# One streaming-encoder layer on one core: w_out's load and split, the sample's output tile and bank L's release are put later in the last stage

## The chip, the cores and the metric

The kernel runs on one core of a Trainium2 chip. The metric is the device time of one launch in microseconds (us), median of three runs. A profiled execution gives the rows below.

## The reference

One layer for two request groups that share weights: a prompt of 2048 frames and a sample of 8 streams with 16 new frames each (cut to what matters):

```python
hq, hf, hi, hgate, fq, fk, fv, fgate, fflog, mq, mgate = _split_in(x @ w_in)
forget = lb + (1 - lb) * sigmoid(hf)
o_hg, hg_new = _hgrn2(state, silu(hq), 1 - forget, hi, log(forget))     # gated recurrence, 4 heads of 128
o_fx = _fox(fq, fk, fv, cumsum(log_sigmoid(fflog + b)))                 # causal softmax attention with a forget bias
o_mem = _cross(mq, mem_k, mem_v)                                        # attention into 256 memory tokens
mix = concat([rmsnorm(o_hg) * silu(hgate), o_fx * silu(fgate), o_mem * silu(mgate)])
y = layernorm(DN_ALPHA * x + mix @ w_out)
```

All in float32. The kernel makes each float32 product from three products of a high and a low part (names ending in h/hi and l/lo).

## The kernel before

The first two thirds of the span project x by w_in (tiles `pj`), spill the results to DRAM (`s_q`, `s_f`, `s_kk` and so on), do the sample's attention and recurrence, and begin the prompt's attention. At about 1009 us of the span the last stage starts. It holds, for 16 tiles of 128 frames: the recurrence (`hgrn_tile`: PSUM banks `L` and `M`, work tile `hQK`, mask tile `hC`), the attention into memory (`cross`: `cqg`, `cP`), the rest of the prompt's attention (`fox`, from the sixth step of its third block of 512 frames on: keys `fk`, queries `fq`, probabilities `fP`, sums `facc`, output `pv`), and the output projection (`out_tile`: bank `o`, weights `woh`/`wol`, row tile `y`), first for the sample ("s", whose mix `ms` POOL fetches from `s_ms`), then for the 16 prompt tiles.

`drive` writes the order of TensorE's work in this stage. Each of those generators is a `Stream`; a `yield` gives the shape of its next matmuls, their planned time, a chain of things that must come first (`("D", 0.7)`: 0.7 us planned on VectorE; `("A", ..)`: ScalarE; `("M", t)`: t us of plain waiting; a third entry names a bank freed when that link ends) and the banks it takes. The plan keeps its own clock and picks a ready stream. It knows neither the DMA queues nor the split of w_out. The order on the other engines is made by the framework from the order of the code and its own planned times; each engine runs its instructions in that order and stops at the first one that has to wait. So does the SP queue with its DMA issues.

One tile of the recurrence does its masked products level by level: three groups of matmuls into `L` (slots 0 and 1 in one group of width 64, then slots 2 and 3), then into `M`. Between two levels VectorE multiplies `hQK` by the running products `P` (L713), and copies the finished slots into `hC` (`pick`, L721 and L723). The forget values `hF` have one buffer: the next tile's are asked for when this tile has used its own. A tile t of the recurrence may begin when output tile t-3 is done (`AHEAD = 3`).

w_out (8 blocks of 128 rows, 512 KB each) comes through the two buffers of `y`, the same ring that `out_tile` uses: each block is cast to `woh` on ScalarE (L1148) and the rest to `wol` on VectorE (L1149), in two halves; block k+2 is asked for when block k is split.

Of the kernel before, what the change touches and what calls it, by code (L numbers as in the profile page):

```python
# [89 lines left out]
def kernel(  # L90
# [185 lines left out]
    def finish(gen):  # L276
        for _ in gen:
            pass
# [403 lines left out]
    def hgrn_tile(t, hb, psh, psl, hstate, emit_mix, bufs, psm=None):  # L682
# [18 lines left out]
        L = psl()  # L701
# [28 lines left out]
        for slot, b in enumerate((2, 4, 8) if smp else (2, 4, 8, 16), 2):  # L730
            P = update(b // 2, P)
            side = [("D", -0.25)] * 2
            if slot == 3:
                pick(0, 1)
                side = [("D", -0.55)]
            elif slot == 4:
                pick(2)
            elif slot == 5:
                pick(3)
            if slot == 5:  # L740
                yield 32, 0.3, [("D", 0.7), ("D", -0.3), ("D", -0.2, "L")], {}
            else:
                yield 32, 0.3, [("D", 0.7), ("D", -0.3)] + side, {"M": 1} if slot == 4 else {}
            if slot == 4:
                M = (psm or psh)()
            for h in range(4):
                for i in range(4):
                    c = slice(32 * i, 32 * i + 32)
                    d = L[c, h, slot, :] if slot < 4 else M[c, h, 32 * slot - 128 : 32 * slot - 96]
                    mm(d, K[:, h, c], Q[:, h, c])  # L750

        if not smp:
            P = update(16, P)
            pick(4)
            yield 32, 0.3, [("D", 0.7), ("D", -0.45)], {}
            for h in range(4):
                for i in (0, 2):
                    c = slice(32 * i, 32 * i + 32)
                    d = slice(32 * i + 32, 32 * i + 64)
                    mm(M[64 + 16 * i : 96 + 16 * i, h, 64:96], K[:, h, c], Q[:, h, d])  # L760
            P = update(32, P)
            pick(5)
            A = diag[t % 2]
            for i in range(4):
                c = slice(32 * i, 32 * i + 32)
                ACT.copy(A[c, :, c], C[c, :, :])
            yield 64, 0.5, [("D", 0.7), ("D", -0.4), ("A", -1.0)], {}
            for h in range(4):
                mm(M[0:64, h, 64:128], K[:, h, 0:64], Q[:, h, 64:128])
            P = update(64, P)  # L770
            ACT.copy(A[0:64, :, 64:128], M[0:64, :, 64:128])
            ACT.copy(A[0:32, :, 32:64], M[64:96, :, 64:96])
            ACT.copy(A[64:96, :, 96:128], M[96:128, :, 64:96])
        else:
            P = update(8, P)
            pick(3, 4)
            A = tl([128, 4, 128], "hA", 1)
            DVE.tensor_tensor(out=A.rearrange("p h (i t) -> p h i t", t=32),
                              in0=C.unsqueeze(2).to_broadcast([128, 4, 4, 32]),
                              in1=bm3.unsqueeze(1).to_broadcast([128, 4, 4, 32]), op=ALU.mult)  # L780
# [203 lines left out]
    def fox(n):  # L984
        T0 = 512 * n
        c0 = T0 if n < 2 else T0 + 128
        for pr in range(2):
            hs = slice(2 * pr, 2 * pr + 2)
            q1 = fp.tile([68, 2, 512], F32R, name="fq1", bufs=1)
            POOL.dma_start(q1[0:64], s_qq[0:64, hs, T0 : T0 + 512])  # L990
            POOL.dma_start(q1[64:68], s_m[:, n, pr])
            q2 = fp.tile([128, 2, 512], F32R, name="fq2", bufs=1)
            POOL.dma_start(q2, s_qq[:, hs, T0 : T0 + 512])
            pv = pf.tile([128, 512], F32, name="pv")
            acc = [fp.tile([128, 512], F32, name=f"facc{hh}", bufs=1) for hh in range(2)]
            def values(V, st, t0, PT, first, last):
                for hh in range(2):
                    r = slice(64 * hh, 64 * hh + 64)
                    mm(pv[r, t0:], V[:, st, r], PT[hh][:, t0:], start=first, stop=last)
                if not first:  # L1000
                    for hh in range(2):
                        DVE.tensor_tensor(out=acc[hh][:, t0:], in0=acc[hh][:, t0:], in1=PT[hh][:, t0:], op=ALU.add)  # L1002

            for c in range(n + 1):
                V = fp.tile([128, 4, 128], F32, name="fV")
                SP.dma_start(V, s_fv[512 * c : 512 * c + 512, 128 * pr : 128 * pr + 128]
                             .rearrange("(j p) c -> p j c", p=128))
                for duo in (0, 2):
                    cs = slice(512 * c + 128 * duo, 512 * c + 128 * duo + 256)
                    k1 = fp.tile([68, 2, 256], F32R, name="fk1", bufs=2)  # L1010
                    POOL.dma_start(k1, s_kk[64:132, hs, cs])  # L1011
                    k2 = fp.tile([128, 2, 256], F32R, name="fk2", bufs=2)
                    POOL.dma_start(k2, s_kk[0:128, hs, cs])
                    PTs, us, wait = [], 0.0, []
                    for st in (duo, duo + 1):
                        t0 = 128 * st if c == n else 0
                        first = c == 0 and st == 0
                        size = (512 - t0) / 512
                        us += size
                        sl = slice(128 * (st % 2), 128 * (st % 2) + 128)  # L1020
                        yield 128, 0.95 * size + 0.1 * (c == n), wait + [("M", 3.0 if first else 0.1)], {"f": 2}
                        PT = []
                        for hh in range(2):
                            ps = ptf()
                            mm(ps[:, t0:], k1[:, hh, sl], q1[:, hh, t0:], start=True, stop=False)
                            mm(ps[:, t0:], k2[:, hh, sl], q2[:, hh, t0:], start=False, stop=(c < n))
                            if c == n:
                                mm(ps[:, t0 : t0 + 128], identb, cstb, start=False, stop=True)
                            pT = acc[hh] if first else fp.tile([128, 512], F32, name="fP", bufs=B_FP)
                            ACT.activation(pT[:, t0:], ps[:, t0:], AF.Exp)  # L1030
                            PT.append(pT)
                        PTs.append((st, t0, PT, first, c == n and st == 3))
                        wait = [("A", 0.1 + 0.5 * size, "f"), ("A", 0.1 + 0.5 * size, "f")]
                    yield 64, 0.95 * us, wait, {}
                    for args in PTs:
                        values(V, *args)
            yield 64, 1.0, [("D", 0.7)] * 3, {"f": 1}, lambda: have["O"] >= 4 * ((2 * n + pr - 3) // 2)
            lp = ptf()
            for hh in range(2):
                mm(lp[64 * hh : 64 * hh + 64, :], ones[:, 0:64], acc[hh])  # L1040
            rl = fp.tile([128, 512], F32, name="fP", bufs=B_FP)
            ACT.activation(rl, lp, AF.Ln)
            ACT.activation(rl, rl, AF.Exp, scale=-1.0)
            DVE.tensor_tensor(out=rl, in0=pv, in1=rl, op=ALU.mult)
            gt = fp.tile([128, 512], F32, name="fP", bufs=B_FP)
            SP.dma_start(gt, s_fg[pr, :, c0 : c0 + 512])
            DVE.tensor_tensor(out=gt, in0=gt, in1=rl, op=ALU.mult)
            mixF[n, pr] = tuple(fp.tile([128, 512], F32R, name=f"mixF{i}", bufs=5) for i in range(2))
            split_mix(mixF[n, pr][0], mixF[n, pr][1], gt)
            yield None, 0.0, [("A", 0.6, "f"), ("A", 0.6), ("D", 0.7), ("D", 0.7), ("A", 0.6), ("D", 0.7)], {}  # L1050
        fox_done[0] = n + 1
# [174 lines left out]
    def out_tile(t):  # L1226
# [14 lines left out]
        for half in range(2):  # L1241
            c = slice(512 * half, 512 * half + 512)
            for k in range(8):
                yield 128, 0.71, [("D", 0.7, "o"), ("D", -0.7)] if half and not k else [], {} if k else {"o": 1}
                if k == 0:
                    ps = ptile("o", B_O)
                mm(ps, lhs(0, k), woh[:, k, c], start=(k == 0), stop=False)
# [76 lines left out]
    def outs():  # L1324
        for t in ["s"] + list(range(16)):
            need["O"] = t
            yield from out_tile(t)
            have["O"] = 0 if t == "s" else t + 1
# [8 lines left out]
    def drive():  # L1337
        h = Stream(hgrn_tiles(0), lambda: busy[0] < have["O"] + AHEAD)
        g = Stream(hgrn_tiles(1), lambda: busy[1] < have["O"] + AHEAD)
        x = Stream(crosses(), lambda: have["C"] < have["O"] + AHEAD)  # L1340
        f = Stream(fox_gen)
        o = Stream(outs(), out_ready)
        shape = 128
        while any(s.live for s in (h, g, x, f, o)):
# [25 lines left out]
    for a in range(2):  # L1370
        for i in range(2):
            POOL.dma_start(ms[a][i], s_ms[i, 4 * a : 4 * a + 4].rearrange("k p t -> p k t"))
    finish(load_w_out())
    with tc.manual_schedule(engines={PE.engine}):
        drive()

# [71 lines left out]
```

## Time and profile before

| what | value |
|---|---|
| median of 3 runs | 1562.55 us (1560.22 to 1562.56) |
| profiled execution, device time | 1558.94 us |
| its span from first to last instruction | 1557.1 us |
| TensorE busy | 1440.6 us (93% of the span) |
| VectorE, ScalarE, GpSimd busy | 755.0, 506.8, 169.3 us |
| mean granted TensorE clock | 0.973 |

Busy time of TensorE is that of pipelined matmuls, so 93% is not 93% of its peak. Idle time of another engine costs nothing unless TensorE comes to wait for it.

### The profile page before, as it was taken

Reading aid. Unit: us, or ns where it says so; the run is one execution under the profiler, and the core shown is the slowest. Engines: PE = TensorE matmul, PEld = TensorE weight load, DVE = VectorE, ACT = ScalarE, POOL = GpSimd, SP = SyncE. Lnnn points to the kernel's source line nnn. Section 1 sums busy time; section 2 is a strip of 40 time slices with the busy share of each in tenths; the row PEclk is TensorE's granted clock in tenths of the full one; section 3 lists DMA queues with packets and bytes.
Section 4 is the critical chain, followed back from the end, with each engine's and each line's share of the span. In section 5 each row is a group of like instructions: output and inputs, shape, how many; then the busy total and the mean of one; then the engine's idle time right before and its main releaser. Section 6 shows DMA issues by size and latency. Waiting matters only on the chain.

```text
span 1557.1 us, 29616 instructions
## 1 busy us (share of the span) xinstructions
PE 1440.6 (93%) x12119; PEld 1170.7 (75%) x12119; DVE 755.0 (48%) x1531; ACT 506.8 (33%) x1168; POOL 169.3 (11%) x221
## 2 busy tenths in 40 slices
PE   7999999999998999889899989869998999999997
PEld 7999997996996688768787976626666766666665
DVE  4522232211333155546565323248776667777664
ACT  4323321311333221121111233346553544555441
POOL 0710000000001110000010023211111011011000
PEclk9999999999999999999999999979999999999999
DMA  7655349568668886585452375594644344444221
GB/s 247 208 146 165 132 161 302 196 202 278 213 224 256 257 251 193 159 248 176 131 144 85 128 161 117 121 242 120 163 112 120 104 108 107 134 107 112 78 76 61
DMA packets 219527, 254.71 MB, mean 164 GB/s; under 512 B 40190, under 2 KB 165310, under 8 KB 219392
## 3 DMA queue, kind: packets, MB, share of 16 engines
q1 hardware_dynamic: 165984, 217.32, 44.3%
q0 software_dynamic: 53408, 35.51, 11.0%
q8 instruction: 95, 1.56, 0.4%
q14 instruction: 40, 0.33, 0.1%
HBM read 199.55 MB, written 53.12 MB: 162 GB/s over the span
## 4 chain that ended last, share of the span: by engine, by line
PE 62%; DMA 17%; DVE 10%; issue 5%; ACT 3%; POOL 2%; SPq 1%; DVEq 0%; ACTq 0%; POOLq 0%
PE pj L122 32%; PE o L122 9%; PE f L122 4%; DMA wraw<-in_w_feat_dram 4%; PE pv L122 3%; PE h L122 3%; DMA rb<-s_r 2%; PE dv L122 2%; PE ds L122 2%; DMA fk<-s_kk 2%; PE M L122 2%; DMA hF<-s_f 2%; DMA xr<-in_x_feat_dram 1%; DVE hQK L713 1%; DMA fq1m<-s_qq 1%
## 5 line engine op out<-in xcount | busy, mean ns | idle before, releaser
L122 PE MATMUL pj<-xh,whi 128*128 128x384 f32 (+1 forms) x1056 | 362.4, 343 | 2.2 <-DVE lo L355 1.4
L122 PE MATMUL pj<-xh,wlo 128*128 128x384 f32 (+1 forms) x1056 | 350.2, 332 | 0.2 <-DVE wlo L262 0.2
L122 PE MATMUL pj<-xl,whi 128*128 128x384 f32 (+1 forms) x1056 | 349.5, 331 | 0.0
L122 PEld LDWEIGHTS pj<-xh,whi 128*128 128x128 f32 x1056 | 201.5, 191 | 27.3 <-issue 19.2
L122 PEld LDWEIGHTS pj<-xl,whi 128*128 128x128 f32 x1056 | 201.3, 191 | 4.8 <-issue 1.2
L122 PEld LDWEIGHTS pj<-xh,wlo 128*128 128x128 f32 x1056 | 200.7, 190 | 3.5 <-issue 2.9
L307 ACT ACTIVATE e<-pj 128x384 f32<-128x384 f32 (+1 forms) x96 | 45.3, 473 | 348.4 <-PE pj L122 307.0
L950 DVE TENSOR_REDUCE fmx<-pj 128x1 f32<-128x512 f32 (+3 forms) x160 | 96.3, 609 | 78.0 <-PE pj L122 77.0
L122 PE MATMUL pj<-whi,xh 128*128 128x256 f32 (+1 forms) x408 | 122.2, 300 | 12.2 <-ACT whi L261 8.6
L262 DVE TENSOR_TENSOR wlo<-wraw,whi 128x1024 fp32r<-128x1024 f32 (+1 forms) x60 | 75.3, 1255 | 117.3 <-ACT whi L261 116.9
L1002 DVE TENSOR_TENSOR facc<-facc,fP 128x512 f32<-128x512 f32 (+3 forms) x144 | 83.1, 600 | 92.1 <-ACT fP L1030 61.3
L122 PE MATMUL pj<-wlo,xh 128*128 128x256 f32 (+1 forms) x408 | 117.8, 289 | 0.2 <-DVE wlo L262 0.2
L122 PE MATMUL pj<-whi,xl 128*128 128x256 f32 (+1 forms) x408 | 117.7, 289 | 0.0
L122 PE MATMUL f<-fq,fk 68*128 68x512 f32 (+4 forms) x320 | 94.6, 408 | 22.6 <-DMA fk<-s_kk 13.6
L122 PEld LDWEIGHTS pj<-whi,xh 128*128 128x128 f32 x408 | 79.3, 195 | 28.0 <-issue 13.7
L261 ACT CAST whi<-wraw 128x1024 fp32r<-128x1024 f32 (+1 forms) x60 | 62.8, 1046 | 106.5 <-DMA wraw<-in_w_feat_dram 100.6
L1030 ACT ACTIVATE fP<-f 128x512 f32<-128x512 f32 (+3 forms) x144 | 72.1, 524 | 75.0 <-PE f L122 74.1
L122 PEld LDWEIGHTS f<-fq,fk 68*128 68x128 f32 (+1 forms) x320 | 56.8, 201 | 41.3 <-issue 13.9
L122 PE MATMUL pj<-fk1m,fq1m 66*128 66x512 f32 (+3 forms) x160 | 64.3, 404 | 19.5 <-DVE fmx L950 9.6
L1011 POOL DMA_DIRECT2D fk<-s_kk x40 | 39.9, 997 | 386.7 <-PE f L122 333.3
L122 PEld LDWEIGHTS pj<-wlo,xh 128*128 128x128 f32 x408 | 79.8, 196 | 1.9 <-issue 0.8
L122 PEld LDWEIGHTS pj<-whi,xl 128*128 128x128 f32 x408 | 79.5, 195 | 1.8 <-issue 0.8
(304 smaller groups left out, 2352.7 us busy)
## 6 DMA issues: line engine op xcount, KB each, us to landing
kv<-in_cache_fox_k_dram SPq DMA_DIRECT2D x64, 512.0 KB
kv<-in_cache_fox_v_dram SPq DMA_DIRECT2D x64, 512.0 KB
wraw<-in_w_feat_dram SPq DMA_DIRECT2D x56, 512.0 KB
fk<-s_kk POOLq DMA_DIRECT2D x40, 256.0 KB, 4.6
xr<-in_x_feat_dram SPq DMA_DIRECT2D x34, 256.0 KB
rb<-s_r SPq DMA_DIRECT2D x32, 256.0 KB
y<-in_x_prompt_dram SPq DMA_DIRECT2D x16, 512.0 KB
out_dram<-y SPq DMA_DIRECT2D x16, 512.0 KB
```

Source lines behind the costliest of these rows:

```text
L122: PE.matmul(out, lhsT=lhsT, rhs=rhs, start=start, stop=stop)
L261: pin(ACT.copy(hi[:, r, :w], raw[:, :, :w]))
L262: pin(DVE.tensor_tensor(out=lo[:, r, :w], in0=raw[:, :, :w], in1=hi[:, r, :w].bitcast(F32), op=ALU.subtract))
L307: ACT.activation(e, ps, AF.Sigmoid)
L713: DVE.tensor_tensor(out=qk, in0=qk, in1=by, op=ALU.mult)
L950: DVE.tensor_reduce(out=mx[:, hh, tt, c : c + 1], in_=ps, axis=AX.X, op=ALU.max)
L1002: DVE.tensor_tensor(out=acc[hh][:, t0:], in0=acc[hh][:, t0:], in1=PT[hh][:, t0:], op=ALU.add)
L1011: POOL.dma_start(k1, s_kk[64:132, hs, cs])
L1030: ACT.activation(pT[:, t0:], ps[:, t0:], AF.Exp)
```

## The change

```diff
             if slot == 5:
-                yield 32, 0.3, [("D", 0.7), ("D", -0.3), ("D", -0.2, "L")], {}
+                yield 32, 0.3, [("D", 0.7), ("D", -0.3), ("D", -0.3)], {}
...
             P = update(16, P)
             pick(4)
-            yield 32, 0.3, [("D", 0.7), ("D", -0.45)], {}
+            yield 32, 0.3, [("D", 0.7), ("D", -0.2, "L"), ("D", -0.3)], {}
...
-                        yield 128, 0.95 * size + 0.1 * (c == n), wait + [("M", 3.0 if first else 0.1)], {"f": 2}
+                        yield 128, 0.95 * size + 0.1 * (c == n), wait + [("M", 6.0 if first else 0.1)], {"f": 2}
...
-                yield 128, 0.71, [("D", 0.7, "o"), ("D", -0.7)] if half and not k else [], {} if k else {"o": 1}
+                yield 128, 0.71, [("D", 0.7, "o"), ("D", -0.7)] if half and not k else [("M", 20.0)] if t == "s" and not k else [],\
+                    {} if k else {"o": 1}
...
         f = Stream(fox_gen)
+        finish(load_w_out())
         o = Stream(outs(), out_ready)
...
-    finish(load_w_out())
     with tc.manual_schedule(engines={PE.engine}):
         drive()
```

Four things: the plan frees bank `L` one level later in a tile; the first step of each head pair of the prompt's attention is planned 6 us instead of 3 us after the one before; the first half of the sample's output tile is planned 20 us after its stream is made (its second half keeps the old chain); and the code that loads and splits w_out stands behind the first steps of the recurrence, cross and attention streams, which issue their first loads.

SP queue, from the last two loads ahead of the stage on (`lng`, `lnb`: the layer norm's weights; `y<-in_w_out_dram`: w_out's blocks; `hQK`, `hV`: tile 1 of the recurrence; `cqg`: tile 0 of cross):

```order
 L1130 DMA lng<-in_ln_g_dram 128x1024
 L1131 DMA lnb<-in_ln_b_dram 128x1024
+L694 DMA hQK<-s_q 128x4x128
+L696 DMA hV<-s_v 128x512
+L1183 DMA cqg<-s_mq 128x2x128
+L1184 DMA cqg<-s_mg 128x2x128
 L1140 DMA y<-in_w_out_dram 128x1024 x2
-L694 DMA hQK<-s_q 128x4x128
-L696 DMA hV<-s_v 128x512
-L1183 DMA cqg<-s_mq 128x2x128
-L1184 DMA cqg<-s_mg 128x2x128
-L850 DMA hG<-s_g 128x4x128
```

The first pair of w_out's blocks moves behind four loads; behind the pair now come `fV`, `hG` and tile 1's `hF`, and only then the second pair. On POOL the order stays: four loads of `ms`, then the `fk` loads.

TensorE at the start of the stage, before:

```order
L122 MATMUL pv<-fP,fV 64x512 x3
L122 MATMUL o<-woh,mixHh 128x512
L122 MATMUL o<-wol,mixHh 128x512
L122 MATMUL o<-woh,mixHl 128x512
L122 MATMUL f<-fq_9411,fk_9590 128x512
L122 MATMUL f<-fq_9414,fk_9592 128x512
```

and with the change:

```order
L122 MATMUL pv<-fP,fV 64x512 x3
L122 MATMUL f<-fq_9411,fk_9542 128x512
L122 MATMUL f<-fq_9414,fk_9544 128x512
...
L122 MATMUL L<-hQK 32x64 x16
L122 MATMUL f<-mkT,cqg 128x256 x4
L122 MATMUL L<-hQK 32x32 x16
L122 MATMUL pv<-fP,fV 64x512 x4
L122 MATMUL L<-hQK 32x32 x16
```

The scores of a new key tile (`fk_9590` before, `fk_9542` now, the same load; eight rows in all, before in two lots of four with `o` rows between) come straight behind `pv`; the sample's first `o` matmul stands 30 rows later than it did.

VectorE in the middle of tile 0's levels, before (`P_9674`, `P_9701`, `P_9735` are the products of its second to fourth update):

```order
L713 TENSOR_TENSOR hQK<-hQK,P_9674 128x2x64x4
L723 COPY_PREDICATED hC<-cb,L 128x128
L1149 TENSOR_TENSOR wol<-y,woh 128x512 x2
L723 COPY_PREDICATED hC<-cb,L 128x128
L1149 TENSOR_TENSOR wol<-y,woh 128x512 x2
L713 TENSOR_TENSOR hQK<-hQK,P_9701 128x2x32x8
L1002 TENSOR_TENSOR facc_9417<-facc_9417,fP 128x512
L1002 TENSOR_TENSOR facc_9418<-facc_9418,fP 128x512
L713 TENSOR_TENSOR hQK<-hQK,P_9735 128x2x16x16
L1250 SCALAR_TENSOR_TENSOR y<-y,o 128x512
```

and with the change (`P_9768` and `P_9790` are the last two updates of tile 0):

```order
L1149 TENSOR_TENSOR wol<-y,woh 128x512 x4
L723 COPY_PREDICATED hC<-cb,M 128x128
L1002 TENSOR_TENSOR facc_9417<-facc_9417,fP 128x512
L713 TENSOR_TENSOR hQK<-hQK,P_9768 128x2x8x32
L723 COPY_PREDICATED hC<-cb,M 128x128
L713 TENSOR_TENSOR hQK<-hQK,hF 128x2x256
L1002 TENSOR_TENSOR facc_9418<-facc_9418,fP 128x512
L1219 TENSOR_TENSOR cqg<-h,cqg 128x256
L1149 TENSOR_TENSOR wol<-y,woh 128x512 x2
L679 TENSOR_TENSOR mixMl<-cqg,mixMh 128x256
L1149 TENSOR_TENSOR wol<-y,woh 128x512 x2
L713 TENSOR_TENSOR hQK<-hQK,P_9790 128x2x4x64
```

Before, the last of the 16 halves of the split stood ahead of tile 0's third update; now the second pair stands ahead of its fifth and the third pair ahead of its sixth update, and the fourth pair behind that, in the levels of tile 1.

## Rows read from the trace of the kernel before

**Rows 1.** The page's slices: the TensorE clock that was granted in each of 40 equal slices of the span (38.9 us each), in tenths, and the mean busy share of the DMA engines.
```profile
PEclk9999999999999999999999999979999999999999
DMA  7655349568668886585452375594644344444221
```

**Rows 2.** Four stretches of the stage: window, its length, busy us (and instructions) of TensorE, its weight loads, VectorE, ScalarE, GpSimd; granted clock, DMA share, GB/s.
```profile
1016.00:1040.00 24.00, 13.71 (x31) 4.66 (x31) 9.65 (x20) 7.91 (x13) 6.38 (x8) 0.78 1.12 275
1040.00:1060.00 20.00, 16.90 (x237) 10.42 (x238) 17.14 (x34) 13.81 (x31) 1.71 (x2) 0.76 0.56 166
1060.00:1500.00 440.00, 412.63 (x4646) 295.93 (x4642) 310.75 (x676) 217.47 (x647) 45.00 (x55) 0.98 0.41 112
1500.00:1557.00 57.00, 45.38 (x364) 34.73 (x364) 32.42 (x56) 12.68 (x43) 0.00 (x0) 0.98 0.18 65
```

**Rows 3.** TensorE's instructions in order of time from 1025 us on: start, us, line, tile, count, and in brackets the idle time before and what ended it.
```profile
1025.25 1.93 PE L122 MATMUL pv<-fP,fV 128*64 128x512 f32 x6
1027.94 0.49 PE L122 MATMUL o<-woh,mixHh 128*128 128x512 f32 x1 [0.76 <-ACT woh L1148]
1028.67 0.49 PE L122 MATMUL o<-wol,mixHh 128*128 128x512 f32 x1 [0.23 <-DVE wol L1149]
1029.46 0.49 PE L122 MATMUL o<-woh,mixHl 128*128 128x512 f32 x1 [0.30 <-DMA mixHl<-s_ms]
1037.31 0.80 PE L122 MATMUL f<-fq,fk 68*128 68x512 f32 x1 [7.36 <-DMA fk<-s_kk]
1039.20 1.65 PE L122 MATMUL f<-fq,fk 128*128 128x512 f32 x3 [1.09 <-DMA fk<-s_kk]
...
1046.63 0.46 PE L122 MATMUL L<-hQK 128*32 128x32 f32 x32 [0.50 <-DVE hQK L713]
1047.44 0.50 PE L122 MATMUL o<-woh,mixHh 128*128 128x512 f32 x1 [0.36 <-ACT woh L1148]
1048.51 0.50 PE L122 MATMUL o<-wol,mixHh 128*128 128x512 f32 x1 [0.56 <-DVE wol L1149]
...
1050.06 0.79 PE L122 MATMUL o<-woh,mixHh 128*128 128x512 f32 x1 [0.82 <-ACT woh L1148]
...
1052.80 0.66 PE L122 MATMUL L<-hQK 128*32 128x32 f32 x32 [0.79 <-DVE hC L723]
...
1066.94 0.40 PE L122 MATMUL o<-woh,mixHh 128*128 128x512 f32 x1
1067.18 0.39 PE L122 MATMUL o<-wol,mixHh 128*128 128x512 f32 x1
```

**Rows 4.** VectorE's instructions in order of time, the same columns.
```profile
1027.92 2.50 DVE L1149 TENSOR_TENSOR wol<-y,woh 128x512 fp32r<-128x512 f32 x4 [1.24 <-DMA hQK<-s_q]
1040.66 0.69 DVE L1002 TENSOR_TENSOR facc<-facc,fP 128x512 f32<-128x512 f32 x1 [10.24 <-ACT fP L1030]
```

**Rows 5.** The issues of the `fk` loads on POOL in order of time, and what the instructions of line 1013 (the larger of the two loads of a key tile) show from issue to landing in 1015 to 1045 us.
```profile
1020.28 1.01 POOL L1011 DMA_DIRECT2D fk<-s_kk  x1
1021.28 0.73 POOL L1013 DMA_DIRECT2D fk<-s_kk  x1
DMA to landing us min/median/max: 15.9/16.9/17.9
```

**Rows 6.** SP's DMA issues in order of time.
```profile
1017.73 1.03 SPq L1140 DMA_DIRECT2D y<-in_w_out_dram  x2
...
1027.22 0.36 SPq L1006 DMA_DIRECT2D fV<-s_fv  x1
1029.24 15.73 SPq L1140 DMA_DIRECT2D y<-in_w_out_dram  x4
1046.60 0.38 SPq L695 DMA_DIRECT2D hF<-s_f  x1
```

**Rows 7.** The DMA queues in 1016 to 1040 us (q1 is SP's, q0 is POOL's): packets, MB, share of 16 engines; and the size of a w_out issue and of an `hF` issue in the list of issues.
```profile
q1 hardware_dynamic: 3513, 4.81, 73.1%
q0 software_dynamic: 3647, 1.77, 39.1%
y<-in_w_out_dram SPq DMA_DIRECT2D x8, 512.0 KB
hF<-s_f SPq DMA_DIRECT2D x17, 256.0 KB
```

**Rows 8.** A piece of the chain that ended last: start, us, what.
```profile
1044.64 4.73 DMA y<-in_w_out_dram
```

**Rows 9.** The stretches of 4 us in which the granted clock fell a second time, columns as in rows 2.
```profile
1048.00:1052.00 4.00, 2.67 (x5) 1.08 (x5) 3.02 (x7) 2.14 (x5) 0.00 (x0) 0.68 0.70 224
1052.00:1056.00 4.00, 3.21 (x39) 2.66 (x39) 3.82 (x13) 3.88 (x9) 0.66 (x1) 0.50 0.35 131
```

**Rows 10.** What TensorE waited for in 1060 to 1557 us: who, for whom, us in total, times, longest.
```profile
PE L L122 <- DVE hC L723: 26.4, 14, 4.8
PE o L122 <- DVE y L1250: 3.4, 7, 0.9
PE M L122 <- DVE hC L723: 0.9, 2, 0.5
PE h L1209 <- ACT hkT L787: 0.2, 1, 0.2
```

**Rows 11.** All engines in order of time around the longest of those waits.
```profile
1187.35 0.70 DVE L713 TENSOR_TENSOR hQK<-hQK,hF 128x512 f32<-128x512 f32 x1
...
1195.28 0.69 DVE L697 TENSOR_TENSOR hQK<-hQK,hF 128x512 f32<-128x512 f32 x1 [4.00 <-DMA hF<-s_f]
1198.08 0.66 PE L122 MATMUL L<-hQK 128*32 128x32 f32 x32 [4.82 <-DVE hC L723]
```

## The prediction

> **What bounds the kernel now.** The granted clock over the span comes first: one slice of forty is below 9 tenths, and there the DMA engines are at their busiest of the last third [rows 1]. It is the start of the last stage, the place that the change touches. Next the stage by stretches: from 1016 to 1040 us TensorE is busy 13.71 of 24 us at a clock of 0.78, from 1040 to 1060 us 16.90 of 20 at 0.76; after that it is 94% busy (412.63 of 440) at 0.98 [rows 2]. So the stage is TensorE's, with a hole of some 13 us at its start and small waits behind. TensorE's rows in order of time tell what the hole is: the last `pv` is through at 1027.2, three `o` matmuls of the sample follow with short waits on the split of w_out, and then it waits 7.36 and 1.09 us for a key tile `fk`; from 1046 to 1053 us come five more waits, three on the split (0.36, 0.56, 0.82) and two in the recurrence (0.50, 0.79) [rows 3]. The `fk` load had been issued at 1021.28 and took 15.9 to 17.9 us [rows 5], because 6.6 MB moved in those 24 us at 275 GB/s [rows 2, 7]. VectorE stood idle for 10.24 us for the same load, after it had split w_out's first pair of blocks in 2.50 us [rows 4]. Last the waits of the rest: 26.4 us in 14 waits of an `L` group on `hC`, 3.4 us on `y`, 1.1 us others [rows 10].
>
> **Bank L's release.** It moves a planned time, so only rows in TensorE's order. The 26.4 us look as if they were meant, but one wait for each of the 14 tiles left says something else: it is the third `L` group of a tile, behind its own tile's first two `pick`s, not the next tile's first group. The plan lets a tile begin when an output tile ends, so two tiles overlap in `L` only at the start of the stage. I take 0 for the 14 waits (bounds: 26.4 gained if they did follow the release, 0), since nothing ahead of the third group is edited.
>
> **The fox wait of 6.** It puts a head pair's first scores 3 us later in the plan, past other matmuls that are ready. Among the waits after 1060 us none is on a query or key load [rows 10], so there is nothing to gain; other work covers it: 0.
>
> **w_out and the sample's tile.** Seven terms, all against the profiled execution (1558.94 us, span 1557.1, 1.84 around it); the sum is a difference and is then put on the median, 1562.55, which lies 3.6 above.
>
> 1. Three waits for the split inside 1047 to 1051 us go, since no `o` stands there: 0.36 + 0.56 + 0.82 = -1.7 [rows 3]. The waits ahead of the first three `o` (0.76, 0.23, 0.30) gain nothing: TensorE then waits for `fk` from 1027.2 instead of 1029.9.
> 2. `fk` lands earlier. Its issue is the same (POOL's order is unchanged). On SP the first pair of w_out's blocks still is asked for before `fk` lands, but the second pair, 1.0 MB issued from 1029.24 on [rows 6], now waits for a split that ScalarE reaches only behind the cross scores. In its place come tile 1's `hF`, 0.25 MB [rows 7]. 0.75 MB at 275 GB/s is 2.7 us [rows 2]; the other bound is 0, if the second pair's bytes were mostly behind `fk`'s. I take -2.2, as the issue at 1029.24 is 10 us ahead of the landing.
> 3. The three `o` matmuls done inside the wait come later, in busy time: 3 x 0.23 us at full clock (start to start, [rows 3]) = +0.7.
> 4. The first split, 2.50 us on VectorE [rows 4], leaves idle time and comes into a stretch where VectorE is busy 17.14 of 20 us [rows 2]. Bounds 0 (TensorE is the limit there) and +2.5; I take +1.5, nearer the upper, since VectorE is that full.
> 5. New waits. ScalarE and VectorE keep their order, and VectorE's rows now have the second pair's split ahead of tile 0's fifth update and the third pair's ahead of its sixth. A block is asked for when its buffer is split and takes 4.73 us [rows 8]; the recurrence's updates and the `P` behind them stand meanwhile. Lower bound: 0, if VectorE's other rows between two splits (10 to 20 of 0.3 to 0.7 us) fill the 4.73. Upper bound: two whole landings, 9.5, less the recurrence's waits that they replace here (0.50 + 0.79 [rows 3]) = 8.2. Following the rows by hand with those durations, I find TensorE stopping about 2.5 us at the last `M` group of tile 0 and 2 us at its transposes, against 1.3 plus smaller ones now: I take +1.2, much nearer the lower bound.
> 6. The clock. It fell a second time in 1048 to 1056 us, to 0.68 and 0.50, which is 1.2 GHz in the latter, after the waits of point 1. At the higher level the 2.67 and 3.21 us of work would take 0.32 x 2.67 + 0.5 x 3.21 = 2.5 us less [rows 9]. Bounds -2.5 (no second fall) and +2.5 (one more such stretch while only the recurrence and attention feed TensorE): I take -1.0.
> 7. The rest of the stage gets another order. The largest wait in it, 4.82 us, is made by VectorE standing 4.00 us at the next tile's `hQK` (L697), whose `hF` landed late, with this tile's update behind it [rows 11]; the other 13 average (26.4 - 4.82) / 13 = 1.66 [rows 10]. Bounds -3.2 (it does not come back) and +3.2 (a second one): I take -1.5, half of the gain, as the new order has places alike.
>
> Sum: -1.7 - 2.2 + 0.7 + 1.5 + 1.2 - 1.0 - 1.5 = -3.0. On the median that is **1559.5 us**; on the profiled execution 1556.
>
> A rule on the second term. In 1016 to 1040 us the two queues moved nearly the same number of packets, 3513 and 3647, and very unequal bytes, 4.81 and 1.77 MB [rows 7]. The Trainium skill, page "DMA: Bandwidth & Descriptors", section "Queues, rings and completion order", says that each DMA engine takes turns between the queues it has work for, a packet at a time; the trace agrees, with these counts. By that rule POOL's queue is slowed by the packets that SP's puts between its own, not by all that is outstanding; the packets ahead of the second pair are the same ones in another order, so the landing would move by nearly 0 and the sum would be -0.8, 1561.8 us, inside the forecast's own range below.
>
> **Rivals.** *Slower.* The split becomes a chain of four landings in which ScalarE and VectorE stand still. Place: VectorE's row of tile 0's sixth update, behind the third pair. It decides when TensorE comes to that tile's transposes before the third pair has landed. For it: VectorE's rows above; against: there is other work in between. Price: point 5 at +6 instead of 1.2, point 2 at 0, point 6 at +1: -1.7 + 0.7 + 1.5 + 6 + 1 - 1.5 = +6.0, so 1568.5. *A larger gain.* Keys land as if the first pair were behind them too: another 1.0 MB, 3.8 us; the second fall of the clock goes (-2.5 instead of -1.0), the rest as summed: -3.0 - 3.8 - 1.5 = -8.3, so 1554. For it: the pair is issued some 4 us later; against: still 14 us ahead of the landing. *Nothing moves.* VectorE is the limit from 1040 to 1070 us and works off the same rows, whatever TensorE waits for: points 1 and 6 come back as other waits, points 2 and 4 cancel: 1562.5.
>
> **How the numbers follow.** A measurement of this kernel can tell 0.2%, 3.1 us, from no change. The forecast has 0.44, with its own range 1556 to 1564, half of it under 1559.4; slower 0.25; larger gain 0.17; nothing moves 0.14. Faster: 0.44 x 0.52 + 0.17 = 0.40; same: 0.44 x 0.46 + 0.13 = 0.33; slower 0.27. The range leaves out the far ends of the slower case and of the larger gain: 1551 to 1568.
>
> **What would show it.** Right: TensorE's wait for `fk` begins at about 1027 and ends at 1035 to 1038; no wait on `woh` or `wol`; `L` on `hC` still once a tile, 22 to 28 us in total; the granted clock above 0.9 from 1045 us on. Wrong: `fk` landing at 1039 or later (point 2); ScalarE or VectorE idle for 3 us or more on `y<-in_w_out_dram` with TensorE waiting on `hQK` or `P` behind it (point 5); two or more waits for `hF` of 4 us (point 7); a clear fall of the 26.4 us, which would mean that the release of `L` does what its name says.

## The result and the profile after

The changed kernel takes **1579.5 us** (median of 4 executions, 1573.4 to 1583.5) against 1561.9 us before (median of 4, 1560.2 to 1562.6): 1.0105 times as long, 95% interval [1.0070, 1.0141]. It is slower by 17.6 us; the prediction had 1559.5 us and a range that ended at 1568. The profiled execution of after took 1583.5 us (span 1581.7).

The same four windows as [rows 2], of the kernel after, with the last one up to the end of its span:
```profile
1016.00:1040.00 24.00, 12.53 (x29) 3.78 (x29) 7.14 (x16) 6.45 (x11) 6.39 (x8) 0.84 1.21 272
1040.00:1060.00 20.00, 15.79 (x199) 9.34 (x199) 14.29 (x28) 13.19 (x30) 1.92 (x3) 0.69 0.34 92
1060.00:1500.00 440.00, 401.94 (x4392) 286.97 (x4394) 300.24 (x645) 211.46 (x616) 44.78 (x55) 0.96 0.42 113
1500.00:1581.70 81.70, 67.09 (x660) 51.41 (x656) 50.51 (x96) 23.71 (x80) 0.00 (x0) 0.98 0.20 71
```
The loss isn't at the start of the stage alone. From 1060 to 1500 us TensorE is busy 401.94 us at a clock of 0.96, against 412.63 at 0.98 before: 10.7 us less busy time in 440, at a lower clock.

A sum over the whole stage closes the account. Its start is the same instruction in both (the first `f<-facc` group: 1008.66 us before, 1011.89 after), and from there to the end of the span stand 548.4 us before and 569.8 after, +21.4. TensorE is busy 494.6 us before and 500.1 after with the same 5285 matmuls, which is the clock: +5.5. What TensorE waits for by name adds up to 45.3 and 61.8 us: +16.5. Together +22.0 for the 21.4.

TensorE's waits of after from 1060 us to the end, which answer to [rows 10]:
```profile
PE L L122 <- DVE hC L723: 31.8, 14, 4.8
PE o L122 <- DVE y L1251: 5.1, 10, 1.1
PE h L784 <- DVE hQK L713: 2.9, 1, 2.9
PE h L854 <- DVE hon L848: 2.6, 1, 2.6
PE M L122 <- DVE hC L723: 2.5, 3, 1.6
PE h L1209 <- DVE hon L848: 0.3, 1, 0.3
```
No row is the price of one event: `L` on `hC` grows by 5.4 us over its 14 waits, `o` on `y` by 1.7, and two waits on `hQK` and `hon` are new. Such a wait can be paid twice, in itself and in the clock behind it. TensorE at 1268 us of after, then the stretches of 4 us around that wait (TensorE's busy time, granted clock, DMA share, GB/s):
```profile
1268.36 0.66 PE L122 MATMUL L<-hQK 128*32 128x32 f32 x32 [4.83 <-DVE hC L723]
1264.00:1268.00 4.00, 0.00 (x0) 0.95 0.32 105
1268.00:1272.00 4.00, 3.64 (x39) 0.50 0.23 82
1272.00:1276.00 4.00, 4.00 (x77) 0.70 0.00 0
```
Behind 4.83 us of waiting the clock is at 0.50, its lower level (1.2 GHz), and then at 0.70: by these rows 3.64 x 0.5 + 4.00 x 0.30 = 3.0 us more. Summed in this way over all stretches of 4 us from 1060 us on, the clock's falls cost 8.5 us before and 16.6 us after.

What makes so long a wait is the episode of [rows 11] again, here by way of ScalarE. ScalarE and VectorE of after, in order of time:
```profile
1264.62 0.63 ACT L698 ACTIVATE hQK<-hF 128x512 f32<-128x512 f32 x1 [2.71 <-DMA hF<-s_f]
1266.19 0.18 DVE L1200 RECIPROCAL cl<-cl 128x4 f32<-128x4 f32 x1 [2.35 <-ACT cP L1198]
1266.88 0.69 DVE L713 TENSOR_TENSOR hQK<-hQK,P 128x512 f32<-128x512 f32 x1
```
ScalarE stands for the next tile's `hF`; the exponentials of the cross scores are queued behind it, VectorE stands for their sum (`cl`), and behind that is this tile's update, for which TensorE waits. The prediction allowed for one such episode more or less, 3.2 us either way.

At the start of the stage, TensorE of after (answers to [rows 3]):
```profile
1029.00 1.93 PE L122 MATMUL pv<-fP,fV 128*64 128x512 f32 x6
1038.68 0.79 PE L122 MATMUL f<-fq,fk 68*128 68x512 f32 x1 [7.75 <-DMA fk<-s_kk]
1050.73 0.46 PE L122 MATMUL L<-hQK 128*32 128x32 f32 x32 [2.25 <-DVE hC L723]
1052.99 1.22 PE L122 MATMUL f<-fq,fk 68*128 68x512 f32 x2 [1.14 <-ACT cP L1198]
1061.35 0.38 PE L122 MATMUL M<-hQK 128*32 128x32 f32 x11 [1.61 <-DVE hC L723]
1069.64 1.12 PE L784 MATMUL h<-cb,hQK 128*128 128x128 f32 x4 [2.92 <-DVE hQK L713]
```
SP's issues of after (answers to [rows 6]), and ScalarE and VectorE at the third pair of w_out's blocks:
```profile
1023.42 1.85 SPq L1140 DMA_DIRECT2D y<-in_w_out_dram  x2
1031.38 0.56 SPq L850 DMA_DIRECT2D hG<-s_g  x1
1045.39 0.36 SPq L695 DMA_DIRECT2D hF<-s_f  x1
1052.26 9.17 SPq L1140 DMA_DIRECT2D y<-in_w_out_dram  x4
...
1067.04 1.14 ACT L1148 CAST woh<-y 128x512 fp32r<-128x512 f32 x2 [1.33 <-DMA y<-in_w_out_dram]
1067.69 1.29 DVE L1149 TENSOR_TENSOR wol<-y,woh 128x512 fp32r<-128x512 f32 x2 [1.52 <-ACT woh L1148]
```
The waits on `woh` and `wol` are gone. In their place stand waits on the recurrence and the cross scores, whose rows on ScalarE and VectorE are now behind the split; the last one, 2.92 us, is the chain of the slower rival: w_out's blocks late, ScalarE waiting (1.33 us), VectorE behind it (1.52 us), the recurrence's update behind that.

### The profile page after: what moved, and what is told of

Same layout as the page of the kernel before. It is cut to its first block, busy times and chain, and to the rows that moved or that the text cites. A ratio compares the mean times of both kernels' runs of the same rounds, so it can differ in the third digit from the quotient of the medians.

```text
span 1581.7 us, 29626 instructions
## 1 busy us (share of the span) xinstructions
PE 1447.9 (92%) x12119; PEld 1175.8 (74%) x12119; DVE 757.4 (48%) x1531; ACT 509.3 (32%) x1168; POOL 169.2 (11%) x221
## 5 line engine op out<-in xcount | busy, mean ns | idle before, releaser
L307 ACT ACTIVATE e<-pj 128x384 f32<-128x384 f32 (+1 forms) x96 | 45.3, 473 | 355.4 <-PE pj L122 327.0
L122 PE MATMUL f<-fq,fk 68*128 68x512 f32 (+4 forms) x320 | 97.8, 420 | 20.5 <-DMA fk<-s_kk 13.0
L261 ACT CAST whi<-wraw 128x1024 fp32r<-128x1024 f32 (+1 forms) x60 | 62.8, 1047 | 103.7 <-DMA wraw<-in_w_feat_dram 95.5
```

Source lines behind the costliest of these rows:

```text
L122: PE.matmul(out, lhsT=lhsT, rhs=rhs, start=start, stop=stop)
L261: pin(ACT.copy(hi[:, r, :w], raw[:, :, :w]))
L307: ACT.activation(e, ps, AF.Sigmoid)
```

## The experiments

One kernel's executions turned out to lie some 20 us apart: 1553.5 to 1572.8 us in 31 executions of the kernel before on one chip. So each verdict goes by the ratio to executions of before on the same chip, with its 95% interval; a trace shows one execution only, and is read for the stage alone (from the first `f<-facc` to the end). In the table "waits" is TensorE's idle time in the stage as far as the trace names what ended it. The only trace of the wait of 6 alone is of an execution of 1585.4 us, the longest of its eleven, and is left out.

| kernel | median us | ratio | stage us | TensorE busy | waits |
|---|---|---|---|---|---|
| before | 1561.3 to 1563.7 | 1 | 548.4 | 494.6 | 45.3 |
| bank L | 1561.6 | 1.0009 [0.9972, 1.0046] | 552.5 | 497.3 | 47.2 |
| wait of 6 | 1571.9 | 1.0059 [1.0026, 1.0091] | | | |
| bank L, wait of 6 | 1570.0 | 1.0033 [0.9998, 1.0069] | 562.0 | 502.4 | 51.7 |
| w_out and tile | 1574.5 | 1.0072 [1.0039, 1.0105] | 561.5 | 495.8 | 57.4 |
| w_out and tile, wait of 6 | 1581.4 | 1.0121 [1.0089, 1.0154] | 565.8 | 500.0 | 57.6 |
| w_out and tile, bank L | 1560.5 | 0.9988 [0.9951, 1.0026] | 547.2 | 491.2 | 47.9 |
| all (after) | 1579.5 | 1.0105 [1.0070, 1.0141] | 569.8 | 500.1 | 61.8 |

**Two halves.** Theory A: the loss lies in the order of the whole stage, which the two numbers (L's release, the fox wait) shift. Theory B: it lies in the split of w_out between the mixers' first rows. First the numbers without w_out (here and below only the changed parts of the lines):
```
-  [("D", 0.7), ("D", -0.3), ("D", -0.2, "L")]      +  [("D", 0.7), ("D", -0.3), ("D", -0.3)]
-  [("D", 0.7), ("D", -0.45)]                       +  [("D", 0.7), ("D", -0.2, "L"), ("D", -0.3)]
-  ("M", 3.0 if first else 0.1)                     +  ("M", 6.0 if first else 0.1)
```


> Kernel before with two of the four parts: bank L freed one level later and the fox wait of 6 instead of 3; w_out is asked for and split as before, and the sample's tile stands as before. Theory A (the loss is made by the order of the whole stage, which these two numbers shift): most of the loss, 1572 to 1580 us, with L on hC above 30 us in the stage. Theory B (the loss is made by the split of w_out between the mixers' first rows on ScalarE and VectorE): 1559 to 1565 us, L on hC near the 27.2 us of before.

Then w_out and the tile without the numbers (the load can't be moved alone, as the program would wait on itself, so these two are not told apart):
```
-    finish(load_w_out())
     with tc.manual_schedule(engines={PE.engine}):
         drive()
...
         f = Stream(fox_gen)
+        finish(load_w_out())
-  [("D", 0.7, "o"), ("D", -0.7)] if half and not k else []
+  [("D", 0.7, "o"), ("D", -0.7)] if half and not k else [("M", 20.0)] if t == "s" and not k else []
```


> Kernel before with the other two parts: w_out asked for behind the mixers' first loads, and the sample's tile 20 us later; bank L and the fox wait as before. Theory A: 1559 to 1566 us, and the waits on hQK, fP and cP at 1030 to 1075 us cost no more than the 8 us of waits that they replace. Theory B: 1572 to 1580 us, with the waits of the changed kernel at the start of the stage (pv on fP, h on hQK, f on cP, L on hC) there again, and L on hC longer in the rest because the stage begins out of step.

Measured: +0.33% [-0.02, +0.69] and +0.72% [+0.39, +1.05]. The second half loses, the first at most a part; neither makes all of it, so neither theory stands as it was put. Next the whole change less one number at a time.

> The changed kernel with bank L freed where before freed it. If L's later release makes the loss (a part of theory A): 1560 to 1566 us and L on hC near 27 us. If it does nothing (prediction's step, 0): 1573 to 1583 us. Theory B: 1573 to 1583 us too.

> The changed kernel with the fox wait back at 3. If the wait of 6 makes the loss (the other part of theory A): 1560 to 1566 us. If it does nothing (prediction's step, 0): 1573 to 1583 us. Theory B: 1573 to 1583 us too.

With L freed as before the loss stays (+1.21%). With the fox wait back at 3 it is gone: 0.9988 [0.9951, 1.0026], and the stage takes 547.2 us, as before. So **without the wait of 6 this change loses nothing**, and w_out with its waits at the start costs nothing that can be measured where L is released later and the wait is 3. The two numbers by themselves on the kernel before:

> Kernel before with the fox wait of 6 alone. Theory M1 (the later first scores of a head pair take work away from between the recurrence's steps, wherever the kernel is otherwise changed): 1568 to 1576 us, with waits of 2.5 us or more on hon, hQK or hC between 1350 and 1410 us that before has not, and TensorE's busy time in the stage 5 us or more above the 494.6 of before through a lower granted clock. Theory M2 (the value does nothing by itself; each new order of the stage meets by chance a few waits of 4 us or not): 1558 to 1580 us, and no such place in common.

> Kernel before with bank L freed one level later alone. Prediction's step (0): within 4 us of before. Theory M1: L matters only where it moves a whole piece of the order: 1558 to 1568 us, and the loss of the two together (6.5 us) is that of the wait of 6. Theory M2: anything between 1550 and 1575 us.

L alone does nothing, as predicted; the wait of 6 alone costs 0.59%, 9 us. M1 has its time.

The eight kernels of the table price each part in four surroundings; a difference of two ratios carries some 0.5% of noise. The wait of 6 costs 0.59% on the kernel before, 0.24 with bank L, 0.49 with w_out and the tile, 1.17 with both: it is the one part that comes out as a cost in all four. w_out and the tile cost 0.72% on the kernel before, 0.62 with the wait of 6, 0.72 with the wait and bank L, and -0.21 with bank L alone. So the wait is not the whole of it: leaving out w_out and the tile instead brings the change down to +0.33%.

**Other values.** The same line with 4.0 and with 2.0, all else as in after:

> The changed kernel with the fox wait at 4 instead of 6 (3 gave 1560.5 us, 6 gives 1579.5). Theory M1: a third of the way or more, 1564 to 1576 us. Theory M2: no order by the value; it may lie on either side of both.

> The changed kernel with the fox wait at 2. Theory M1: no slower than with 3, 1553 to 1562 us. Theory M2: no order by the value; as 3 is one order among many, more likely slower than it, 1562 to 1580 us.

4 gives 1569.3 us, 1.0068 [1.0031, 1.0106]; 2 gives 1576.2 us, 1.0089 [1.0056, 1.0122]. So 2, 3, 4 and 6 give 1576, 1560, 1569 and 1580: a step away from 3 costs on both sides. M1 fails at 2, and M2's "no order by the value" stands. So there is no price for each us of planned waiting; each value gives another order of work, and what is lost has to be looked for in that order. For 6 this is done below, for 2 and 4 not.

**Where it lies.** The wait of 6 for some head pairs only, here the last two (late); in the other kernel (early) the two values are exchanged:
```
+  ("M", (6.0 if 2 * n + pr >= 6 else 3.0) if first else 0.1)
```


> The changed kernel with the fox wait of 6 only for the last two head pairs (their first scores come after 1235 us), 3 for those before. Theory P (place: the wait of 6 costs where it empties single places between the recurrence's steps, and these lie late, at 1268, 1307, 1364 and 1410 us): 1571 to 1578 us, the waits on hon and hC of 2.5 us and more at those places again and more falls of TensorE's clock than with 3. Theory E (the early ones put the stage out of step and the rest follows): 1558 to 1566 us.

> The opposite: 6 only for the head pairs whose first scores come before 1235 us, 3 for the last two; TensorE's order differs from that with 3 throughout (1560.5 us) only between about 1095 and 1235 us. Theory P: 1560 to 1567 us, one wait of 4 us at 1180 at most. Theory E: 1571 to 1579 us, with the later places losing although their rows stand as in the faster kernel.

Late: 1578.1 us, 1.0098 [1.0067, 1.0129]. Early: 1568.2 us, 1.0035 [1.0005, 1.0065]. Against the 0.9988 with 3 throughout, the late two carry the larger part, 1.1%. The early ones are not free: 0.47%, 1 us above theory P's 1560 to 1567, and in their trace the stage takes 558.9 us. With the late wait of 6 it takes 562.1 us and with 3 throughout 547.2 (the latter execution began its stage 13.0 us later, so its rows carry later times).

The first place where the two orders part, TensorE's rows up to the tile's third `L` group, with the late wait of 6:
```profile
1239.95 0.66 PE L784 MATMUL h<-cb,hQK 128*128 128x128 f32 x4
...
1244.43 1.18 PE L122 MATMUL f<-fq,fk 68*128 68x512 f32 x4
...
1248.64 1.10 PE L122 MATMUL f<-fq,fk 68*128 68x512 f32 x4
...
1261.06 0.66 PE L122 MATMUL L<-hQK 128*32 128x32 f32 x32 [4.92 <-DVE hC L723]
```
and with 3 throughout:
```profile
1249.20 1.10 PE L122 MATMUL f<-fq,fk 68*128 68x512 f32 x4
1250.13 0.60 PE L784 MATMUL h<-cb,hQK 128*128 128x128 f32 x4
...
1254.56 1.18 PE L122 MATMUL f<-fq,fk 68*128 68x512 f32 x4
...
1260.86 1.10 PE L122 MATMUL f<-fq,fk 68*128 68x512 f32 x4
...
1269.69 0.46 PE L122 MATMUL L<-hQK 128*32 128x32 f32 x32 [2.31 <-DVE hC L723]
```
With 3 the head pair's first four `f` matmuls stand ahead of the transposes (L784), and three such groups come before the third `L` group; with 6 the first comes behind the transposes and there are two. TensorE has one group, 1 us, less to do, and arrives while ScalarE still stands for the next tile's `hF` (2.81 us up to 1257.32; with 3 it doesn't stand at all). The wait is 4.92 us instead of 2.31, and the clock is at 0.54 from 1260 to 1264 us (with 3, at 0.75 from 1268 to 1272). Behind it the two orders stay apart: 1.81 us on `hon` at 1355.55, where with 3 there is no wait, and then the third `L` group of a later tile. With the late wait of 6:
```profile
1387.57 1.94 PE L122 MATMUL pv<-fP,fV 128*64 128x512 f32 x8
1391.28 0.65 PE L122 MATMUL L<-hQK 128*32 128x64 f32 x32
...
1400.24 0.66 PE L122 MATMUL L<-hQK 128*32 128x32 f32 x32 [3.47 <-DVE hC L723]
```
and with 3 throughout:
```profile
1391.25 0.65 PE L122 MATMUL L<-hQK 128*32 128x64 f32 x32
...
1392.89 1.94 PE L122 MATMUL pv<-fP,fV 128*64 128x512 f32 x8
...
1399.61 0.46 PE L122 MATMUL L<-hQK 128*32 128x32 f32 x32 [1.22 <-DVE hC L723]
```
With 3 eight `pv` matmuls, 1.94 us, stand between the tile's first and third group; with 6 they stand ahead of the first, and the wait is 2.25 us longer. The other traces repeat it. With the `pv` behind the first group the third waits 1.20 to 1.41 us (before, w_out and tile, the same with bank L, early); where the wait of 6 has put them ahead it waits 3.35 to 3.47 (after, w_out and tile with the wait of 6, late). So M2's "no such place in common" does not hold for 6. Other orders of this tile (bank L alone, the values 4 and 2) have no `pv` there either and wait 1.6 to 1.8 us, and bank L with the wait of 6 has them there and waits 4.22: it is the order around the group that counts, not one row of it.

These three places make 6.7 us; over the stage TensorE's waits are 55.7 us with the late wait of 6 and 47.9 with 3, 7.8 more, and its busy time for the same matmuls is 498.6 and 491.2 us, 7.4 more, which is the clock.

**What holds the third `L` group.** It is the largest wait of both kernels. The group needs its update on VectorE (`hQK`, L713), but it writes the bank that the picks of slots 0 and 1 read, and stands behind them in the program. VectorE of the kernel before, then TensorE:
```profile
1252.16 0.68 DVE L713 TENSOR_TENSOR hQK<-hQK,P 128x512 f32<-128x512 f32 x1
1252.76 0.28 DVE L721 TENSOR_TENSOR hC<-L,cb 128x128 f32<-128x128 f32 x1
1252.96 0.68 DVE L1002 TENSOR_TENSOR facc<-facc,fP 128x512 f32<-128x512 f32 x1
1253.56 0.17 DVE L1200 RECIPROCAL cl<-cl 128x4 f32<-128x4 f32 x1
1253.65 0.27 DVE L723 COPY_PREDICATED hC<-cb,L 128x128 f32<-128x128 uint32 x1
1253.97 0.51 PE L122 MATMUL L<-hQK 128*32 128x32 f32 x32 [2.36 <-DVE hC L723]
```
The update is through at 1252.84; the group starts at 1253.97, behind two picks and two rows of attention and crosses between them. So the picks were written behind the group, with the plan and TensorE's order as they were:
```
             if slot == 3:
-                pick(0, 1)
                 side = [("D", -0.55)]
...
                     mm(d, K[:, h, c], Q[:, h, c])
+            if slot == 3:
+                pick(0, 1)
```


> Kernel before with one thing of the recurrence changed: the picks of slots 0 and 1 are written behind the third L group instead of ahead of it, so that this group no longer follows them; TensorE's order is the same. If the 28 us of waits of L on hC are there because the group has to follow two picks that it doesn't need, with other rows of VectorE between them (0.3 to 1.1 us in each of 14 waits): L's waits fall to 12 to 20 us, fewer falls of the clock, 1545 to 1558 us. If the group really waits for its update (hQK) and the picks are only the last named: no change, 1558 to 1564 us, the same waits under the name hQK.

> The same edit of the picks in the changed kernel with the fox wait at 3. If the picks hold the group: 1542 to 1556 us. If not: 1557 to 1564 us, as without the edit.

On the kernel before: **1543.1 us, 0.9876 [0.9828, 0.9923]**, faster than both kernels of this case. On the changed one with the wait of 3: 1546.2 us, 0.9898 [0.9847, 0.9948]. What TensorE waits for in `L` in the first of them from 1060 us on, and the group at the place shown above:
```profile
PE L L122 <- DVE hQK L713: 12.8, 12, 3.5
1249.99 0.46 PE L122 MATMUL L<-hQK 128*32 128x32 f32 x32 [1.24 <-DVE hQK L713]
```
26.4 us have become 12.8, at this place 2.36 have become 1.24, and the clock's falls from 1060 us on cost 1.5 us instead of 8.5. The stage takes 533.9 us instead of 548.4: over the whole of it TensorE waits 11.1 us less (34.2 against 45.3) and is busy 3.2 us less (491.4 against 494.6). The Trainium skill, page "PSUM — Partial Sum Buffer", section "Terms", says that TensorE writing and VectorE reading the same bank and quadrant at once is an error. Written either way one stands behind the other, and no run here lets them meet.

**Does the loss pass through these waits?** The same edit on the whole change:

> The changed kernel, whole (fox wait 6, L freed later, w_out behind), with the edit of the picks. Theory V (the change loses because its order leaves less other work ahead of groups that have to follow VectorE's picks; the loss is in those waits and in the clock's falls behind them): the loss against the unchanged parameters shrinks with them: 1545 to 1555 us, 2 to 12 us above the 1543.1 of the same edit in the kernel before, and L's waits within 5 us of its 12.8. Theory O (the order is worse by itself, whatever holds the third group: waits on hF, hon, hQK, cP): the loss stays near 17 us: 1557 to 1564 us.

1561.6 us, 1.0014 [0.9985, 1.0043]: 18 us above the same edit on the kernel before. Theory O stands in its time: the loss does not need the held group. Against the same edit with the wait of 3 (0.9898) the wait of 6 costs 1.16%, as much as without the edit (1.17%). The stage takes 547.1 us against 533.9; 12.4 of these 13.2 us are waits (46.6 against 34.2), spread over `L` on `hQK` (18.5 against 12.8), `M`, `hon`, `cP` and `y`.

## Why the prediction was wrong

**The step that failed: "The fox wait of 6 ... there is nothing to gain; other work covers it: 0."** It was priced by the one wait that it could shorten, a load of keys or queries, of which [rows 10] have none. What it takes away was not asked: the scores themselves are the cover of the recurrence's waits. Planned three us later, they and the `pv` behind them come at other places between the recurrence's steps, and the places that they leave are bare: 4.92 us of waiting for 2.31 and 3.47 for 1.22 at the two `L` groups shown. Alone the wait of 6 measures 0.59% (9 us), on top of the other parts 0.9988 to 1.0105 (some 18 us). The prediction also priced the parts one by one and added them; w_out and the tile cost 0.72% or nothing, by the order around them.

**Bank L, 0:** right alone (1.0009). It isn't nothing in the other order: w_out and the tile lose 0.72% without it and nothing that can be measured with it. That its 14 waits have nothing to do with the release was right; what they do hang on, two picks ahead of the group, could be read from the order of the rows and was taken as given.

**Point 1**, the split's waits in 1047 to 1051 us: gone, as said. **Point 2**, `fk` earlier by 2.2: right. From issue to landing, the later of the two loads took 17.9 us [rows 5] and takes 15.9 now; it took 16.3 to 18.9 in four other kernels with w_out ahead, and 14.7 to 16.0 in ten with w_out behind. (From the end of `pv` to the first `f`, TensorE's hole was 10.1 us before, 1027.18 to 1037.31 [rows 3], and is 7.75 now, but it also hangs on when `pv` ends: 4.2 to 9.3 us in those ten.) The "nearly 0" that was worked out beside the Trainium skill's rule of turns ("DMA: Bandwidth & Descriptors", "Queues, rings and completion order") counted the packets ahead of the second pair as the same ones; the second pair's own no longer follow them, and nothing comes in their place: behind `hG` at 1031.38 SP asks for nothing until 1045.39. Point 3 can't be told apart in these traces.

**Points 4 and 5**, the split in a busy stretch and new waits, +2.7 together: too small. From 1041 to 1091 us TensorE's waits add up to 9.4 us of after (on `hQK` 2.9, `hC` 2.2 and 1.6, `cP` 1.1 and 0.5, `y` 1.1), against 2.9 in the same 50 us of before without the split's 1.8: +6.5. The rival "slower" had the chain, of which 2.9 us lie at the place that it named, and with 1.5 + 6 nearly the size of these two points; its 1568.5 us for the whole is still 11 us short. **Point 6**, one fall of the clock less: wrong, the clock is 0.69 in 1040 to 1060 us instead of 0.76, with falls behind the new waits. **Point 7**, -1.5 with 3.2 either way: wrong in sign, and the bound was made from one episode, where the whole order had changed: `L`'s waits alone rose by 5.4 us, the clock's falls from 1060 us on by 8.1.

With the wait at 3 and L released later, the seven points' part of the change measures -0.12% (0.9988) where -0.2% was predicted. That agreement is luck in good part: points 4 to 6 were too low, and the rest of that kernel's stage has no wait of 4.8 us, which the stage of before does. Under the wait of 6 the same part costs 0.72% (1.0033 to 1.0105).

**Still open:** why 2 loses nearly as much as 6, what the early head pairs' 0.47% are made of, and why w_out and the tile lose 11 us with L's old release. Of the latter's 14.3 us in the stage (561.5 against 547.2) 11.5 are there by the third `L` group at 1213.68 us (205.7 us into its stage; 194.2 with L released later, at 1215.64); the trace has 4.60 us at 1142.76 in front of it, behind a late `hF`, but that episode wasn't taken out by itself. A late `hF`, which has one buffer, also stands at the head of the longest waits of before (4.82), after (4.83) and late (4.92); a second buffer for it was not tried.

## What to carry to other kernels

A planner's waiting time is not priced by the wait that it is meant to save: ask which instructions it moves, and which waits of other chains these covered until now. Where one group waits in every tile, put the end of the input that it needs beside its start; what stands between them is the price of the order in the program, and moving it (here two picks, 1.2%) was worth more than any of the planned times tried here, of which the best stays level with the kernel before. A plan tuned to one set of numbers answers to any new number with a new order, so test the parts alone and together, since they need not add up: w_out and the tile cost 0.72% and bank L 0.09, but the two together -0.12.

## What the runs showed that was not expected

The spread of one kernel's executions is wide on one core: 31 of the kernel before lie between 1553.5 and 1572.8 us on one chip, and the granted clock goes with it (1552.5 us of span at 0.975, 1570.7 at 0.967). The three executions that were shown ahead of the prediction (1560.2 to 1562.6) hid that; ten executions of a kernel against 31 of before still leave intervals of 0.35% to either side, so the 0.2% that the prediction took for measurable was too fine.

A wait of less than 2 us can be followed by a fall of the clock, and one as long need not be: in after the 1.75 us ahead of 1375.64 is followed by this, while behind 1.68 us ahead of 1367.24 in the kernel with the late wait of 6 the clock stays at 1.00 (TensorE's busy time and clock, after first):
```profile
1376.00:1380.00 4.00, 4.00 (x56) 0.60 0.43 137
1368.00:1372.00 4.00, 4.00 (x83) 1.00 0.45 137
```
So small waits carried much of the clock's falls here: with each cut from 1.9 to 1.1 us on the average (26.4 / 14, 12.8 / 12) the falls from 1060 us on went from 8.5 to 1.5 us.
